# When the weights' high and low planes are made in an encoder block's projections: 20 and 26 products behind the load instead of 24 and 54

## The chip, the cores and the metric

The kernel runs on one core of a Trainium2 chip. Its time is the device time of one execution in microseconds (us). Five engines work side by side, each through its own list of instructions in order, and they wait for each other through semaphores: TensorE (PE in the profile; PEld is its weight load), VectorE (DVE), ScalarE (ACT), GpSimd (POOL) and SyncE (SP), which issues most of the DMAs.

## The reference

One transformer encoder block in float32, for 1024 tokens of width 1024. What matters here is its first half: a layer norm, one wide projection into queries, keys, values and two gates, and two attentions that are computed from it.

```python
h = layer_norm(x, ln0_g, ln0_b)
proj = h @ w_in + b_in                      # 1024 x 1024 times 1024 x 4352
qa, ka, va, qb, kb, vb, ga, gb = split(proj)
y_na = neighbourhood_attention(qa, ka, va, na_rpb) @ w_branch_na     # 8 heads, 16 x 64 grid
y_swa = windowed_gqa_with_sink(rotary(qb), rotary(kb), vb, sink) @ w_branch_swa   # 8 heads, window 128
mixed = sigmoid(ga) * y_na + sigmoid(gb) * y_swa
h = layer_norm(ALPHA * h + mixed @ w_out + b_out, ln1_g, ln1_b)
u = square(relu(h @ w_ff1 + b_ff1))
out = layer_norm(ALPHA * h + u @ w_ff2 + b_ff2, ln2_g, ln2_b)
```

## The kernel before, in words

**Products in two planes.** PE multiplies a rounded type. To keep float32 accuracy, each operand is split into a high plane (the value rounded) and a low plane (value minus high plane), and each product is made as three matmuls: high by high, high by low, low by high. For weights, ScalarE makes the high plane `whi` with a cast (line 550) and VectorE makes the low plane `wlo` with a subtract (line 555).

**Blocks.** The projections are cut into blocks of 128 output columns by all 1024 tokens. A block is 48 products (8 slices of the inner dimension, 3 products each, for two halves of the tokens), issued by `gemm3_steps` (line 282; its matmul is line 288), one for each `next` of a generator. `fills` (line 735) lists the 24 blocks: key, value and first queries of the windowed attention, then its other queries with three gates between, then values, query and key pairs of the neighbourhood heads, and last three more gates. The accumulated 128 x 512 results lie in PSUM under the tag `mm`, two banks, and are evacuated by ScalarE and VectorE.

**Loading a block's weights.** `blocks` (line 539) runs them one behind the other. When a block starts, it forces whatever is not yet made of its own planes, issues the load of the next block's weights (`raw`, 512 KB, two buffers, line 156, on SP's queue) and notes the next block's cast and subtract as deferred steps. `whi` and `wlo` have two buffers each.

```python
            def both():
                split_hi()
                split_lo()
            defer(D_W[0], split_hi, D_W[1], split_lo)
            return both
        force = {0: fetch(0)}
        yield
        for j, (_, run) in enumerate(todo):
            force[j]()
            if j + 1 < len(todo):
                force[j + 1] = fetch(j + 1)
            yield from run(got[j])
```

**Deferred steps.** `defer(n, f, m, g)` (line 295) puts f on a list with a counter of n. `pump` (line 788) issues products and lowers all counters by one for each. `flush` (line 299) runs those whose counter has come to zero, and only then puts g on the list with a counter of m. So m counts from the place where f ran, and a step whose count is up still waits for the next flush. The code is written in the order in which the engines get their instructions; nothing is moved later.

**Where the products run.** The first 188 products (`N_PRE`, line 874) run with a flush after every 4. The others fill the attention's 64 steps and two more: 12 products in a step for the first eight heads (windowed), 18 for the other eight (neighbourhood), 4 steps a head. `steps` (line 849) writes a step s in this order: scores of step s + 2 (`part_a`: four matmuls, lines 606 and 607, into the banks `s` and `t`; VectorE adds the mask and takes the maximum in line 608, then lines 613 or 615), 25% of the products, an early flush for some evacuations, the low half of the probabilities of step s + 1 (`part_l`: VectorE line 643, then a transposing DMA, line 646, into `pt`), exponentials of step s + 2 (`part_e`: ScalarE lines 631 and 634), a flush, 45% of the products, the value matmuls of step s - 1 (`part_c`: line 716 out of `pt`, evacuated by lines 722 and 725), a flush, and the remaining products. With 12 products the parts are 3, 5 and 4, with 18 they are 4, 8 and 6. One rotary operation on GpSimd (lines 458 to 462) is put behind each step's scores while there are any; lines 506 and 511 split its result. Lines 662, 664 and 687 belong to the softmax's normalisation, once for two heads.

After this stage come the rest of the gates, the branch products, the output projection, and the two MLP products (matmuls of lines 1419 and 1852), which the change does not touch.

Of the kernel before, what the change touches and what calls it, by code (L numbers as in the profile page):

```python
# [44 lines left out]

B_V = 8
N_AHEAD = 4
D_W = 24, 30
D_NA = 4
D_ROPE = 4, 22, 8  # L50
D_ROPE2 = 4, 40, 4
# [37 lines left out]
def encoder_block(ctx, tc, x, w_in, w_br, w_out, w_ff1, w_ff2, par, rows, rpbp,  # L89
# [205 lines left out]
    def defer(*fns, pe=False, early=False):  # L295

        later.append([fns[0], fns[1:], pe, early])
# [241 lines left out]
    def blocks(todo):  # L539
# [4 lines left out]
        def fetch(j):  # L544
# [7 lines left out]
            def split_lo():  # L552
                if len(got[j]) == 2:
                    got[j].append(0)
                    W_ENG.tensor_tensor(out=got[j][1], in0=raw, in1=b32(got[j][0]), op=ALU.subtract)  # L555
# [6 lines that stand above are left out]
# [1570 lines left out]
```

## Time and profile before

| | us |
|---|---|
| median of 3 runs (lowest, highest) | 1331.54 (1330.53, 1331.69) |
| the profiled execution, its own time | 1329.35 |
| its span, first to last instruction | 1327.5 |
| PE busy in the span | 1276.8 |
| VectorE, ScalarE, GpSimd busy | 945.8, 708.7, 293.5 |
| stretch from 44 to 450 us: PE busy of 406 | 371.89 |

The mean granted clock of PE over the span was 0.985 of full speed. The stretch from 44 to 450 us holds the projections' blocks and the attention's steps. In the profile's rows, a line number is that of the kernel, `out<-in` names the tiles, `x16` is a count, and what stands behind `<-` in brackets or behind `|` is the idle time just ahead and what ended it. Rows of waits give us in total, times, and the longest. Matmuls overlap: one lasts 0.39 us by the profile and the next starts 0.23 us after it.

### The profile page before, as it was taken

The page shows a single profiled execution, that of the slowest core. Times are in us where ns is not written, and L with a number is a line of the kernel's source. Part 1 is how long each engine was busy: PE and PEld are TensorE (multiplying, and loading weights), DVE is VectorE, ACT ScalarE, POOL GpSimd, SP SyncE. Part 2 cuts the span into 40 slices and gives each one's busy share as a digit, 9 for nine tenths or more (in the row PEclk, how much of TensorE's full clock was granted, in tenths as well). Part 3 has the DMA queues.
Part 4 walks back from the last instruction along what each step waited for, and adds up shares of the span by engine and source line. Part 5 has one row for each costly group of instructions (what it writes and reads, how often), then busy time and mean ns, then how long its engine had stood idle before and what let it go on. Part 6 is the DMA issues. An engine that isn't in the chain of part 4 may idle for free.

```text
span 1327.5 us, 16368 instructions
## 1 busy us (share of the span) xinstructions
PE 1276.8 (96%) x5912; PEld 1042.7 (79%) x5912; DVE 945.8 (71%) x1368; ACT 708.7 (53%) x1148; POOL 293.5 (22%) x279
## 2 busy tenths in 40 slices
PE   8998889899999999999999999999999999999997
PEld 6776767677777878888888888888888888888885
DVE  7766666767776896443688986677655768787778
ACT  6446657666766545541446755555555533333346
POOL 4442220212211000344630012222100001111207
PEclk9999889899999999999999999999999999999998
DMA  6525544555455633655233566565528644544323
GB/s 228 190 95 135 114 122 114 120 120 138 124 111 142 191 131 103 215 194 202 80 143 140 193 222 205 207 207 186 202 96 309 222 191 151 214 151 180 121 104 127
DMA packets 167730, 213.64 MB, mean 161 GB/s; under 512 B 110561, under 2 KB 112353, under 8 KB 161889
## 3 DMA queue, kind: packets, MB, share of 16 engines
q1 hardware_dynamic: 166816, 211.81, 49.2%
q8 instruction: 46, 0.75, 0.2%
q10 hardware_dynamic: 832, 0.79, 0.2%
q14 instruction: 36, 0.29, 0.1%
HBM read 130.69 MB, written 56.18 MB: 141 GB/s over the span
## 4 chain that ended last, share of the span: by engine, by line
PE 84%; DVE 10%; ACT 2%; issue 2%; POOL 1%; DMA 0%; DVEq 0%; POOLq 0%
PE ps_mm L288 17%; PE ps_mm L1419 7%; PE ps_o L1419 6%; PE ps_t L1419 6%; PE ps_mm L1852 6%; PE ps_s L1852 6%; PE ps_o L1852 5%; PE ps_t L1852 5%; PE ps_s L1419 3%; PE ps_o L716 3%; DVE wlo L555 2%; PE ps_mm L949 1%; DVE ss L608 1%; PE ps_s L1310 1%; PE ps_s L1309 1%
## 5 line engine op out<-in xcount | busy, mean ns | idle before, releaser
L288 PE MATMUL ps_mm<-hT,whi 128*128 128x512 f32 x832 | 275.1, 405 | 2.6 <-POOL hT L260 2.1
L288 PE MATMUL ps_mm<-hT,wlo 128*128 128x512 f32 x416 | 170.9, 411 | 35.1 <-DVE wlo L555 34.1
L288 PEld LDWEIGHTS ps_mm<-hT,whi 128*128 128x128 f32 x832 | 159.8, 193 | 35.4 <-POOL hT L260 3.5
L288 PEld LDWEIGHTS ps_mm<-hT,wlo 128*128 128x128 f32 x416 | 80.5, 193 | 54.4 <-DVE wlo L555 41.0
L631 ACT ACTIVATE ss<-ss,sk 128x384 f32<-128x384 f32 (+1 forms) x128 | 74.4, 582 | 80.5 <-DVE sk L613 44.6
L1718 ACT CAST t<-stg 128x2048 fp32r<-128x2048 f32 x28 | 53.5, 1912 | 84.2 <-PE ps_o L1852 46.7
L1871 POOL TENSOR_TENSOR acc<-acc,rst 128x512 f32<-128x512 f32 x16 | 29.5, 1841 | 294.1 <-DMA rst<-xr_d 279.4
L1852 PE MATMUL ps_mm<-t,t 128*128 128x512 f32 x384 | 89.7, 389 | 0.0
L1852 PE MATMUL ps_s<-t,t 128*128 128x512 f32 x384 | 89.6, 389 | 0.0
L1852 PEld LDWEIGHTS ps_s<-t,t 128*128 128x128 f32 x384 | 72.1, 188 | 14.9
L1852 PEld LDWEIGHTS ps_mm<-t,t 128*128 128x128 f32 x384 | 72.1, 188 | 15.0
L1419 PE MATMUL ps_t<-hS,tw 128*128 128x512 f32 x348 | 83.6, 389 | 0.0
L1721 DVE TENSOR_TENSOR t<-stg,t 128x2048 fp32r<-128x2048 f32 x28 | 68.7, 2454 | 13.1 <-ACT t L1718 13.1
L1419 PEld LDWEIGHTS ps_t<-hS,tw 128*128 128x128 f32 x348 | 65.3, 188 | 13.5
L1241 POOL TENSOR_TENSOR mx<-sg 128x512 f32<-128x512 f32 x16 | 33.5, 2091 | 176.3 <-DVE sg L1240 176.3
L1852 PE MATMUL ps_t<-t,t 128*128 128x512 f32 x288 | 67.8, 390 | 0.8 <-DVE t L1721 0.8
L1852 PE MATMUL ps_o<-t,t 128*128 128x512 f32 x288 | 67.2, 389 | 0.0
L1695 POOL TENSOR_TENSOR rst<-rst,rr 128x512 f32<-128x512 f32 x16 | 23.3, 1458 | 188.2 <-DMA rst<-xn_d 118.9
L1852 PEld LDWEIGHTS ps_t<-t,t 128*128 128x128 f32 x288 | 53.9, 188 | 12.7 <-DVE t L1721 1.6
L1852 PEld LDWEIGHTS ps_o<-t,t 128*128 128x128 f32 x288 | 54.1, 188 | 11.2
L643 DVE SCALAR_TENSOR_TENSOR pl<-ss,pl 128x640 f16<-128x640 f32 (+1 forms) x64 | 58.3, 912 | 0.3 <-issue 0.2
L1610 DVE TENSOR_TENSOR usl<-usl 128x512 f32<-128x512 f32 x64 | 50.2, 784 | 11.5 <-ACT usl L1503 10.6
(315 smaller groups left out, 2963.3 us busy)
## 6 DMA issues: line engine op xcount, KB each, us to landing
us_d<-usl SPq DMA_DIRECT2D x112, 256.0 KB, 2.6
stg<-us_d SPq DMA_DIRECT2D x28, 1024.0 KB, 4.9
raw<-in_w_ff SPq DMA_DIRECT2D x36, 512.0 KB, 5.4
raw<-in_w_in SPq DMA_DIRECT2D x28, 512.0 KB, 4.1
sg<-sg_d SPq DMA_DIRECT2D x32, 256.0 KB, 3.3
w2b<-in_w_ff SPq DMA_DIRECT2D x7, 1024.0 KB, 7.0
w2a<-in_w_ff SPq DMA_DIRECT2D x5, 1024.0 KB, 6.9
sg_d<-sa SPq DMA_DIRECT2D x16, 256.0 KB, 2.2
```

The costliest lines, as they stand in the source:

```text
L288: PE.matmul(ps, a[:, k, :], act(b, k), start=(k == 0 and i == 0), stop=(k == NK - 1 and i == 2))
L555: W_ENG.tensor_tensor(out=got[j][1], in0=raw, in1=b32(got[j][0]), op=ALU.subtract)
L631: ACT.activation(p, p, AF.Exp, bias=nm[:, i:i + 1], scale=0.125, accum_out=sums_l[o_chunk][:, hh, 2 * t + i:2 * t + i + 1])
L643: DVE.scalar_tensor_tensor(out=pl[:, n:2 * n], in0=e[:, 0:n], scalar=P_SCALE, in1=pl[:, 0:n], op0=ALU.mult, op1=ALU.subtract)
L716: PE.matmul(o, vs, move(part), start=(m == 0 and part == 0), stop=(m == len(runs) - 1 and part == 1))
L1241: POOL.tensor_tensor(out=mx[:, f, half * 512:(half + 1) * 512], in0=both[0], in1=both[1], op=ALU.add)
L1419: PE.matmul(ps, ww, act[:, part, k, :], start=(first and k == 0 and m == 0), stop=(k == 3 and m == 2), skip_group_check=True)
L1610: DVE.tensor_tensor(out=out, in0=a, in1=b, op=op)
L1718: ACT.copy(slot[:, :, 0, :], src)
L1721: DVE.tensor_tensor(out=slot[:, :, 1, :], in0=src, in1=b32(slot[:, :, 0, :]), op=ALU.subtract)
L1852: PE.matmul(ps, st[:, a, part, j * P:(j + 1) * P], w[:, a, wpart, :], start=(first and a == 0 and m == 0), stop=(a == 3 and m == 2), skip_ ...
L1871: POOL.tensor_tensor(out=z, in0=z, in1=t, op=ALU.add)
```

## The change

One tuple of constants. Its first number counts the products from the issue of a block's load to the cast (high planes), the second those from there to the subtract (low planes).

```diff
-D_W = 24, 30
+D_W = 20, 6
```

The low planes were due 24 + 30 = 54 products behind the load and are now due 20 + 6 = 26 behind it. Everything else is as it was.

## The prediction

> **What bounds the kernel now.** I read the page's totals and chain first, then its groups, then the waits of TensorE, and last the instructions around single waits.
>
> ```profile
> span 1327.5 us, 16368 instructions
> PE 1276.8 (96%) x5912; PEld 1042.7 (79%) x5912; DVE 945.8 (71%) x1368; ACT 708.7 (53%) x1148; POOL 293.5 (22%) x279
> ...
> PE 84%; DVE 10%; ACT 2%; issue 2%; POOL 1%; DMA 0%; DVEq 0%; POOLq 0%
> ...
> L288 PE MATMUL ps_mm<-hT,wlo 128*128 128x512 f32 x416 | 170.9, 411 | 35.1 <-DVE wlo L555 34.1
> ```
>
> PE carries the span: busy 96%, 84% of the chain. 1327.5 - 1276.8 leaves 50.7 us of idle PE, and one group holds 35.1 of it: the products that use a low plane, ended by the subtraction of line 555, which makes that plane. Asked for PE alone, from 44 to 450 us (the stage that D_W governs), the waits give one row only, and the line's own view says how many instructions stand behind it:
>
> ```profile
> PE ps_mm L288 <- DVE wlo L555: 34.1, 16, 3.6
> ...
> L555 DVE TENSOR_TENSOR wlo<-raw,whi x24: 1160/1218/2306, 43.6 to 430.1; 128x1024 fp32r<-128x1024 f32 x24
> ...
> L550 ACT CAST whi<-raw x24: 1031/1037/1056, 42.5 to 425.8; 128x1024 fp32r<-128x1024 f32 x24
> ```
>
> So 16 of 24 blocks of 48 products begin with PE idle, 34.1 us in all. Why does VectorE come late? The subtract is due 24 + 30 = 54 products behind the load, but the next block starts 48 behind it and forces it there, two products before its first use. It then stands in VectorE's order behind everything of that step. Here is VectorE around one such place (start, length, what; in brackets idle before it), then PE:
>
> ```profile
> 166.14 0.95 DVE L643 SCALAR_TENSOR_TENSOR pl<-ss,pl 128x768 f16<-128x768 f32 x1
> 167.02 0.74 DVE L458 STREAM_SHUFFLE qs<-qf 128x512 f32<-128x512 f32 x1
> 168.71 0.42 DVE L608 CUSTOM_DVE_ANT_0 ss<-ps_s,bd 128x256 f32<-128x256 f32 x1 [0.95 <-PE ps_s L607]
> ...
> 169.79 0.82 DVE L643 SCALAR_TENSOR_TENSOR pl<-ss,pl 128x640 f16<-128x640 f32 x1
> 170.53 0.68 DVE L725 TENSOR_TENSOR oT<-ps_o,oT 64x512 f32<-64x512 f32 x1
> 171.13 0.78 DVE L662 TENSOR_TENSOR sl<-sl,sk 128x16 f32<-128x16 f32 x1
> ...
> 172.12 1.16 DVE L555 TENSOR_TENSOR wlo<-raw,whi 128x1024 fp32r<-128x1024 f32 x1
> 177.64 0.56 DVE L608 CUSTOM_DVE_ANT_0 ss<-ps_s,bd 128x384 f32<-128x384 f32 x1 [4.37 <-PE ps_s L607]
> ```
>
> ```profile
> 169.78 0.63 PE L288 MATMUL ps_mm<-hT,whi 128*128 128x512 f32 x2
> 173.33 0.50 PE L288 MATMUL ps_mm<-hT,wlo 128*128 128x512 f32 x1 [2.92 <-DVE wlo L555]
> 176.85 0.52 PE L606 MATMUL ps_s<-kh,q 128*128 128x384 f32 x1
> ```
>
> PE ends its two high-plane products at 170.41 and waits 2.92 us while VectorE works through lines 643, 725 and 662 and then the subtract. Straight after that VectorE itself idles 4.37 us, for PE's next scores: the wait is one of order, not of too much work.
>
> A second cost hangs on these waits. The granted clock, in the windows by stretch (us, busy time of PE, PEld, DVE, ACT, POOL, then PEclk, DMA share, GB/s), and the same few PE instructions after a shorter wait:
>
> ```profile
> 40.00:120.00 80.00, 76.27 (x355) 61.67 (x354) 51.65 (x91) 39.59 (x73) 31.52 (x21) 1.00 0.42 134
> ...
> 120.00:400.00 280.00, 250.33 (x1288) 200.32 (x1286) 196.55 (x435) 183.48 (x376) 58.11 (x80) 0.94 0.51 121
> ```
>
> ```profile
> 110.72 0.50 PE L288 MATMUL ps_mm<-hT,wlo 128*128 128x512 f32 x1 [1.78 <-DVE wlo L555]
> 111.05 0.40 PE L288 MATMUL ps_mm<-hT,whi 128*128 128x512 f32 x1
> ...
> 111.88 0.47 PE L288 MATMUL ps_mm<-hT,whi 128*128 128x512 f32 x1
> ...
> 112.88 0.33 PE L606 MATMUL ps_s<-kh,q 128*128 128x384 f32 x1
> ...
> 215.06 0.80 PE L288 MATMUL ps_mm<-hT,wlo 128*128 128x512 f32 x1 [2.30 <-DVE wlo L555]
> ...
> 236.74 0.80 PE L288 MATMUL ps_mm<-hT,wlo 128*128 128x512 f32 x1 [3.57 <-DVE wlo L555]
> ...
> 257.53 0.50 PE L288 MATMUL ps_mm<-hT,wlo 128*128 128x512 f32 x1 [1.84 <-DVE wlo L555]
> ...
> 338.54 0.50 PE L288 MATMUL ps_mm<-hT,wlo 128*128 128x512 f32 x1 [2.56 <-DVE wlo L555]
> ```
>
> From the released product to the next score matmul PE takes 112.88 - 110.72 = 2.16 us after the 1.78 us wait, and 176.85 - 173.33 = 3.52 us after the 2.92 us one. The released product itself shows 0.80 us instead of 0.50 after waits of 2.30 and 3.57. Waits up to 1.84 us show no slow phase; of those from 2.30 us on, most do (2.56 at 338.54 does not). A clock of 0.94 over 280 us is 0.06 x 280 = 16.8 us lost, if PE was busy throughout the slow phases.
>
> **The change, part by part.** One tuple changes: the cast of a block's weights (line 550, ScalarE) is due 20 products behind the load's issue instead of 24, the subtract (line 555, VectorE) 6 behind the cast instead of 30. No work, wait or buffer is added or removed, and loads are issued where they were.
>
> *Where they land.* Deferred steps run only at flushes. In the attention of the first eight heads a step has 12 products, flushed after 3 and 8. The 188 products ahead of the steps put each block's start at the 4th product of a step, so the flushes lie 4, 11, 16, 23, 28, 35, 40, 47 products behind it. The cast moves from 28 to 23. The subtract moves from the next block's start (48) to 35, behind line 643 of the step before. In the later eight heads (18 products a step, flushed after 4 and 12) block starts rotate over products 4, 16 and 10 of a step: the subtract lands at 36, 32 and 30, the cast at 26, 24 (both as before) and 20 (from 30). In the 188 products ahead the flush comes every 4: cast 20, subtract 28.
>
> *The subtract, on VectorE.* Prices on PE:
>
> ```profile
> 96.12 0.17 PE ps_s L606
> ...
> 96.82 2.76 PE ps_mm L288 x12
> ```
>
> A product costs 2.76 / 12 = 0.230 us, a group of four score matmuls about 4 x 0.17 = 0.7, a group of value matmuls 111.88 - 111.05 - 0.23 = 0.6. The low plane is used two products into the next block, 15 or 16 behind its new place, where it was two behind its old one: it gains at least 13 x 0.230 + 0.7 + 0.6 = 4.3 us. The longest wait is 3.6 us, so VectorE may be as late as it is today and every one of the 16 waits still goes. In the step shown, the subtract would come behind the 166.14 instruction, end near 167.1 + 1.2 = 168.3, and be needed at 170.4. Queued behind it there are the shuffle at 167.02 and then the scores of line 608, which have 0.95 us of idle in front; the rest of the delay ends in the following step, which has lost its subtract.
>
> Does VectorE have the room? The sums over seven blocks of the first eight heads, 109.45 to 256.26 us, over six stretches in them without a PE wait, and the idle ahead of the scores:
>
> ```profile
> sum 146.81, PE 126.27 PEld 99.97 DVE 98.85 ACT 94.31 POOL 30.46; mean PE 18.04 PEld 14.28 DVE 14.12 ACT 13.47 POOL 4.35
> ```
>
> ```profile
> sum 71.95, PE 71.95 PEld 58.26 DVE 52.98 ACT 53.44 POOL 14.56; mean PE 11.99 PEld 9.71 DVE 8.83 ACT 8.91 POOL 2.43
> ```
>
> ```profile
> L608 DVE CUSTOM_DVE_ANT_0 ss<-ps_s,bd 128x384 f32<-128x384 f32 x18 | 10.0, 556 | 33.3 <-PE ps_s L607 33.2
> ```
>
> A block takes 146.81 / 7 = 21.0 us, with (146.81 - 126.27) / 7 = 2.9 of waits and, of the slow clock's loss (15, below), some 12 / 7 = 1.7; without both, 16.4. VectorE has 14.1 us of work in it (86%), ScalarE 13.5 (82%). That is tight, but in the stretches without waits VectorE idles 26% and nearly all its idle time (the 33.2 of the last row) is waiting for PE. So little should come back. Bounds: nothing, or, if VectorE could never be busier than the 52.98 / 71.95 = 74% of those stretches, 14.1 / 0.74 = 19.1 us a block, 2.7 more than 16.4, which over 8 blocks is 21 us. I take 4 us, near the lower end, since its idleness is waiting for PE.
>
> *Contention.* One subtract took 2.31 us beside GpSimd work instead of 1.22:
>
> ```profile
> 56.10 1.74 POOL L461 TENSOR_TENSOR qs<-qs,rt 128x512 f32<-128x512 f32 x1
> ```
>
> ```profile
> 56.62 2.31 DVE L555 TENSOR_TENSOR wlo<-raw,whi 128x1024 fp32r<-128x1024 f32 x1
> ```
>
> The subtract ended 58.93, which is GpSimd's end at 57.84 plus 1.1. At its new place it can meet the rotary operations in the same way; 1.1 us more a block is 15.2 of 16.4 on VectorE, still under, and part of why I do not take nothing.
>
> *The cast, on ScalarE.* It costs 1.04 us wherever it stands and ScalarE has 82% at most, so I cost the move at nothing, if the load has landed:
>
> ```profile
> 172.06 0.57 SPq L156 DMA_DIRECT2D raw<-in_w_in  x1
> ```
>
> ```profile
> raw<-in_w_in SPq DMA_DIRECT2D x24, 512.0 KB, 4.1
> ```
>
> The load is issued some 2 us after PE passed the block's start near 170 (SP's queue stood behind a transpose) and lands 4.1 later, 6.2 us after it; 23 products with two score and two value groups take 5.3 + 1.4 + 1.2 = 7.9. In the 188 products ahead, 20 products are 4.6 us: there the cast may wait a little, with the low plane needed only at product 50 (11.5 us). Behind a waiting cast stand exponentials and evacuations; PE gets them a step later. Bound: 0 to 2 us in all; I take 0.
>
> *The slow clock.* If no wait of 2 us is left, its loss goes too: at least 1.36 us (3.52 - 2.16) for each of some eight phases, 11, and at most 16.8. I take 15, nearer to the clock's own row, as phases go on into the scores that my 1.36 cuts off.
>
> *Sum:* 34.1 + 15 - 4 = 45 us. The profiled execution took 1329.35 us, 1.85 around its span; it would take 1284.3. The median shown, 1331.54, is 2.2 above it: 1286.5.
>
> **Rivals.** *VectorE becomes the bound* of the first eight heads: the 21 us above come back as waits on score banks or again on low planes, and about 28 us are left: 1303. For it: 86% busy, in order, up to 1.1 us of contention a split. Against: VectorE's idle time is PE's lateness.
>
> *The clock does not come back*: gain 34 - 4 = 30, time 1301. The slow phases would then be due to something other than these waits. The Trainium skill, "TensorE: Matmul & The Clock Gate", Part 1, has PE drop to half rate after at least one idle window of about 3.4 us. By that rule only the waits near 3.5 us would have slowed it. The trace differs: the 2.30 and 2.92 us waits were followed by slow products, the waits up to 1.84 were not.
>
> *No change*: the subtract, though issued earlier, is executed as late, because the line 643 in front of it waits for ScalarE: 1331. It would need VectorE over 4.3 us later at the new place than at the old.
>
> *Slower*: the value matmuls become late. Line 643 of a step is followed by a transposing DMA, and its values are used two steps later.
>
> ```profile
> pt<-pl SPq DMA_TRANSPOSE x64, 3.2
> ```
>
> Between are 29 products, two score groups and one value group, 6.7 + 1.4 + 0.6 = 8.7 us; line 643 runs about 2.5 us behind PE, takes 1, the DMA 3.2: 6.7. If the subtract in front of the scores makes VectorE more than 2 us later in every step, and not just in one of four, each us beyond is lost 32 times; from 1.5 us beyond it eats the 45 us, at 2 it adds 64 - 45 = 19: 1350. Against: 14.1 us of work in a 16.4 us block does not pile up.
>
> **How the numbers follow.** Forecast 0.68, VectorE-bound 0.17, clock stays 0.05, no change 0.05, slower 0.05. Time 1286.5. The range: down to all 34.1 + 16.8 = 51 us, 1280; up past the VectorE-bound case's 1303 to 1306, which leaves out the last two cases and some tails. A difference of 0.2% (2.7 us) is about what a measurement here can tell from none. Faster 0.68 + 0.17 + 0.05 = 0.90; same 0.05; slower 0.05.
>
> **What would show it.** Right: no wait of PE on line 555 over 0.3 us; the clock 1.00 in the stretches of the first eight heads; a block of those heads 16 to 17 us; VectorE's share there 83 to 88%; idle ahead of line 608 much shorter. VectorE-bound: PE waiting at lines 606 or 288 on 608 or 555, VectorE above 90%. Clock rival: no waits, clock still below 0.97 there. Wrong altogether: PE waits of 2 us or more on line 555 remaining, or the value matmuls (716) waiting for a DMA.

## The result, and the profile after

| | before | changed |
|---|---|---|
| median (lowest to highest), us | 1331.22 (1330.53 to 1331.69), 4 runs | 1282.34 (1281.79 to 1283.22), 4 runs |
| ratio, 95% interval | | 0.9634 [0.9617, 0.9651] |
| profiled execution, its own time / span, us | 1329.35 / 1327.5 | 1281.79 / 1280.0 |
| PE busy / idle in the span, us | 1276.8 / 50.7 | 1259.9 / 20.1 |

The change saves 48.9 us of the median; 1286.5 was forecast. Measured again later, the changed kernel took 1282.81 us, ratio 0.9639 [0.9626, 0.9652].

The page of the changed kernel: totals, chain, and the two groups of products.

```profile
span 1280.0 us, 16384 instructions
PE 1259.9 (98%) x5912; PEld 1033.1 (81%) x5912; DVE 946.0 (74%) x1368; ACT 707.7 (55%) x1148; POOL 295.2 (23%) x279
...
PE 86%; DVE 7%; ACT 3%; issue 2%; DMA 1%; POOL 1%; SPq 0%; DVEq 0%; POOLq 0%
...
L288 PE MATMUL ps_mm<-hT,whi 128*128 128x512 f32 x832 | 269.8, 399 | 6.3 <-DVE kl L401 3.6
...
L288 PE MATMUL ps_mm<-hT,wlo 128*128 128x512 f32 x416 | 165.6, 398 | 1.0 <-DVE wlo L782 1.0
```

The 35.1 us of idle ahead of the low-plane products are down to 1.0, and that is another line. The products themselves are cheaper on average: 398 ns instead of 411. PE's waits in the stage from 44 to 410 us are again a single row, a new one:

```profile
PE ps_mm L288 <- DVE kl L401: 3.6, 6, 1.0
```

The stage splits at the first scores of the neighbourhood heads. The windows of before (first eight heads, other eight), then of the changed kernel:

```profile
91.10:255.20 164.10, 141.98 (x724) 112.88 (x724) 111.08 (x259) 105.42 (x227) 37.24 (x40) 0.92 0.49 115
255.20:445.50 190.30, 178.62 (x938) 144.16 (x937) 138.94 (x293) 124.63 (x249) 35.26 (x56) 0.98 0.53 129
```

```profile
90.50:220.40 129.90, 128.89 (x723) 105.15 (x722) 109.63 (x259) 104.92 (x227) 39.33 (x40) 1.00 0.64 148
220.40:398.10 177.70, 175.04 (x937) 141.60 (x936) 137.95 (x291) 124.49 (x249) 35.30 (x56) 1.00 0.57 136
```

The first eight heads give 34.2 us, the other eight 12.6, together 46.8 of the span's 47.5. In each half idle PE and busy PE can be told apart: idle fell from 22.1 to 1.0 and from 11.7 to 2.7 us (30.1 in all), busy PE by 13.1 and 3.6 (16.7) with the same products, because the clock rose from 0.92 and 0.98 to 1.00. The other engines did the same work, VectorE 111.08 and then 109.63 us, only in less time.

VectorE and PE at the moved subtract, in the same kind of place as the one shown in the prediction:

```profile
134.07 0.95 DVE L643 SCALAR_TENSOR_TENSOR pl<-ss,pl 128x768 f16<-128x768 f32 x1
134.93 1.22 DVE L555 TENSOR_TENSOR wlo<-raw,whi 128x1024 fp32r<-128x1024 f32 x1
136.18 2.39 DVE L511 TENSOR_TENSOR q<-qf,q 64x512 fp32r<-64x512 f32 x2
138.60 0.42 DVE L608 CUSTOM_DVE_ANT_0 ss<-ps_s,bd 128x256 f32<-128x256 f32 x1
...
139.68 0.82 DVE L643 SCALAR_TENSOR_TENSOR pl<-ss,pl 128x640 f16<-128x640 f32 x1
140.53 0.68 DVE L725 TENSOR_TENSOR oT<-ps_o,oT 64x512 f32<-64x512 f32 x1
```

```profile
138.48 0.40 PE L288 MATMUL ps_mm<-hT,whi 128*128 128x512 f32 x1
138.72 0.83 PE L716 MATMUL ps_o<-pt,vv 128*128 128x256 f16 x8
139.31 0.47 PE L288 MATMUL ps_mm<-hT,whi 128*128 128x512 f32 x1
139.62 0.39 PE L288 MATMUL ps_mm<-hT,wlo 128*128 128x512 f32 x1
```

The subtract now follows line 643 of the step before. VectorE is no earlier against PE than before (line 643 of the next step at 139.68, line 725 at 140.53), but PE goes through its products at 139.31 and 139.62 without a gap.

### The profile page after: what moved, and what is told of

It reads as the page before. It is cut to its first block, busy times and chain, and to the rows that moved or that the text cites. A ratio compares the mean times of both kernels' runs of the same rounds, so it can differ in the third digit from the quotient of the medians.

```text
span 1280.0 us, 16384 instructions
## 1 busy us (share of the span) xinstructions
PE 1259.9 (98%) x5912; PEld 1033.1 (81%) x5912; DVE 946.0 (74%) x1368; ACT 707.7 (55%) x1148; POOL 295.2 (23%) x279
## 4 chain that ended last, share of the span: by engine, by line
PE 86%; DVE 7%; ACT 3%; issue 2%; DMA 1%; POOL 1%; SPq 0%; DVEq 0%; POOLq 0%
PE ps_mm L288 17%; PE ps_mm L1419 7%; PE ps_o L1419 7%; PE ps_t L1419 7%; PE ps_mm L1852 7%; PE ps_s L1852 6%; PE ps_o L1852 5%; PE ps_t L1852 5%; PE ps_s L1419 3%; PE ps_o L716 2%; PE ps_mm L949 2%; PE ps_s L1309 1%; PE ps_s L1310 1%; PE ps_s L1308 1%; PE ps_o L279 1%
## 5 line engine op out<-in xcount | busy, mean ns | idle before, releaser
L288 PE MATMUL ps_mm<-hT,whi 128*128 128x512 f32 x832 | 269.8, 399 | 6.3 <-DVE kl L401 3.6
L288 PEld LDWEIGHTS ps_mm<-hT,whi 128*128 128x128 f32 x832 | 155.3, 188 | 40.7 <-ACT ss L631 3.8
L288 PE MATMUL ps_mm<-hT,wlo 128*128 128x512 f32 x416 | 165.6, 398 | 1.0 <-DVE wlo L782 1.0
L631 ACT ACTIVATE ss<-ss,sk 128x384 f32<-128x384 f32 (+1 forms) x128 | 74.3, 582 | 58.3 <-DVE sk L613 34.1
L288 PEld LDWEIGHTS ps_mm<-hT,wlo 128*128 128x128 f32 x416 | 78.4, 188 | 14.1 <-DVE wlo L782 1.5
L1721 DVE TENSOR_TENSOR t<-stg,t 128x2048 fp32r<-128x2048 f32 x28 | 67.6, 2415 | 13.1 <-ACT t L1718 13.1
```

What stands on the lines that cost most here:

```text
L288: PE.matmul(ps, a[:, k, :], act(b, k), start=(k == 0 and i == 0), stop=(k == NK - 1 and i == 2))
L631: ACT.activation(p, p, AF.Exp, bias=nm[:, i:i + 1], scale=0.125, accum_out=sums_l[o_chunk][:, hh, 2 * t + i:2 * t + i + 1])
L1721: DVE.tensor_tensor(out=slot[:, :, 1, :], in0=src, in1=b32(slot[:, :, 0, :]), op=ALU.subtract)
```

## The experiments

My theory was that the whole gain comes from the subtract's place in VectorE's order, directly as waits and through the clock that the waits pull down. The rivals: the earlier cast takes part in it; VectorE's load, not its order, sets the time; the slow clock has another cause. Every edit is shown against the kernel before, unless it says otherwise.

**The cast alone.**

```diff
-D_W = 24, 30
+D_W = 20, 34
```

> The cast alone at 20, the subtract still due 54 behind the load, so still forced at the next block's start. Theory (the whole gain is the subtract's place in VectorE's order): no change, 1331 us within 1.5, PE's waits on line 555 still about 34 us in 16 places, the slow clock still there. Rival (the earlier high planes carry part of the gain, as VectorE's subtract can only start behind the cast): 1320 to 1328 us, shorter waits on line 555.

Measured: 1331.39 us, ratio 1.0006 [0.9996, 1.0015]. PE's waits:

```profile
PE ps_mm L288 <- DVE wlo L555: 34.5, 16, 3.6
```

Same waits, same time: the cast's number has no part in the gain.

**The subtract alone.**

```diff
-D_W = 24, 30
+D_W = 24, 6
```

> The cast as before at 24, the subtract 6 behind it. Theory: the whole gain, 1281 to 1283 us; no wait of PE on line 555. In the later heads the cast of one block in three goes back from 20 to 30 products, so ScalarE no longer waits for the load (6.5 us in the changed kernel), and PE's waits on line 401 (3.6 us there) fall to 2 us or less: perhaps 1 us faster than the changed kernel. Rival (both parts are needed): 1285 to 1300 us.

Measured: 1283.54 us, ratio 0.9652 [0.9637, 0.9666], not to be told from the changed kernel's 0.9634. The whole gain, then, but not the 1 us more that I expected; the time lies just above the theory's 1281 to 1283. ScalarE's 6.5 us of waits for loads are gone, but PE's waits on line 401 fell only from 3.6 to 2.8 us, and two small ones on line 555, where I expected none, remain:

```profile
PE ps_mm L288 <- DVE kl L401: 2.8, 4, 1.1
...
PE ps_mm L288 <- DVE wlo L555: 0.8, 2, 0.5
```

**One flush later.**

```diff
-D_W = 24, 30
+D_W = 20, 13
```

> The subtract 13 instead of 6 behind the cast: in the first eight heads it runs 40 products into the block instead of 35, still ahead of the scores of the step in which the next block starts; in the later heads at 44, 42 and 38. Theory (what counts is that it stands ahead of that step's work in VectorE's order): as the changed kernel, 1282 us within 2, no wait on line 555 over 0.5 us. Rival (only the time by which it is moved ahead comes off each wait, here 8 products and a score group, 2.5 us): 1286 us or more, with waits of 0.3 to 1 us left in six blocks of the first eight heads.

Measured: 1297.16 us, ratio 0.9752 [0.9735, 0.9768]: 15 us slower than the changed kernel and above the theory's 1282 within 2. The rival's "1286 us or more" covers it, but most of the loss is not where the rival had it. The waits on line 555, one of them on PE, and VectorE around it:

```profile
PE ps_mm L288 <- DVE wlo L555: 10.8, 8, 2.6
```

```profile
259.84 0.51 PE L288 MATMUL ps_mm<-hT,wlo 128*128 128x512 f32 x1 [2.56 <-DVE wlo L555]
```

```profile
257.83 0.82 DVE L643 SCALAR_TENSOR_TENSOR pl<-ss,pl 128x640 f16<-128x640 f32 x1
258.57 1.22 DVE L555 TENSOR_TENSOR wlo<-raw,whi 128x1024 fp32r<-128x1024 f32 x1
```

Three waits of 2.56 us stand in the later heads, where I expected none. I had overlooked that for one block in three the flush at 42 lies in the step in which the next block starts, behind that step's line 643. There the wait is 2.56 us, exactly as in the kernel before, although the subtract is issued 6 products earlier. That is the strongest evidence for order: six products buy nothing as long as the same instruction stands in front. In the first eight heads and at their end four small waits are left (0.47 to 0.92 us), fewer than the rival's six, more than the theory's none; there this run does not decide between the two.

**Two flushes later.**

```diff
-D_W = 24, 30
+D_W = 20, 18
```

> The subtract 18 behind the cast: in the first eight heads it runs 47 products into the block, one product ahead of the forced place, behind line 643 of the step in which the next block starts; in the later heads still early, at 44, 42 and 38. Theory: in the first eight heads all waits come back (the nine from 94 to 258 us sum to 24.0 us) with six of the eight slow phases (about 13 us), in the later heads none: 1282.3 + 24 + 13 = 1319 us within 4. Rival (the slow clock and the waits in one part of the stage come from elsewhere, or VectorE's load and not the order makes them): a time near 1282 or near 1331, or waits in both parts.

Measured: 1313.75 us, ratio 0.9877 [0.9862, 0.9892], a little under the 1315 to 1323 of the theory. That it came so near is luck: the theory had 24 us of waits in the first eight heads and none in the later ones, and of the 23.4 us measured, 7.7 are three waits of 2.56 us in the later heads. There the subtract lands at 42 again in one block in three, the place that I overlooked in the run before; waits in both parts were what the rival named. The waits in all, one of them, and VectorE in front of it:

```profile
PE ps_mm L288 <- DVE wlo L555: 23.4, 13, 2.7
```

```profile
167.03 0.51 PE L288 MATMUL ps_mm<-hT,wlo 128*128 128x512 f32 x1 [1.40 <-DVE wlo L555]
```

```profile
165.02 0.82 DVE L643 SCALAR_TENSOR_TENSOR pl<-ss,pl 128x640 f16<-128x640 f32 x1
165.75 1.22 DVE L555 TENSOR_TENSOR wlo<-raw,whi 128x1024 fp32r<-128x1024 f32 x1
166.89 0.68 DVE L725 TENSOR_TENSOR oT<-ps_o,oT 64x512 f32<-64x512 f32 x1
167.49 0.65 DVE L662 TENSOR_TENSOR sl<-sl,sk 128x16 f32<-128x16 f32 x1
```

The subtract comes one product before its forced place, but in the flush it goes ahead of lines 725 and 662, which stood in front of it before. The wait here is 1.40 us where it was 2.92 at the same kind of block start. The difference, 1.5, is about what the two instructions that changed sides took, 0.68 + 0.78. So at this place the wait is, piece by piece, what stands in front of the subtract from line 643 on.

**Filler on PE, no subtract moved.** The kernel before, with eight matmuls in front of nine blocks' first product; they write the bank that this product then starts anew.

```diff
+        filler = 8 if n_half[0] in range(13, 13 + 18, 2) else 0
...
+                for _ in range(filler if k == 0 and i == 0 else 0):
+                    PE.matmul(ps, hi[:, 0, :], act(0, 0), start=True, stop=True)
```

> The kernel before, with 8 filler matmuls (1.84 us) on PE ahead of the first product of the nine blocks that start from 93 to 258 us; they write the bank that the block's first product then overwrites. The low planes are as late as before, so PE is held up to the same moment, only busy instead of idle. Theory (idle PE makes the slow clock): waits left of at most 1.8 us, no slow phase in these blocks, and the 12 to 14 us of slow clock of the first eight heads come back without any subtract being moved: 1318 us within 3. Rival (the slow phases have another cause): 1331 us, or up to 1348 if the fillers do not fit into the waits (9 x 1.84 = 16.6 us more).

Measured: 1319.65 us, ratio 0.9913 [0.9898, 0.9927]: 11.9 us faster, with 72 matmuls more and no operand earlier. The windows of the two halves (the low planes' line is 561 here):

```profile
91.00:244.40 153.40, 145.58 (x788) 117.05 (x788) 111.10 (x259) 105.31 (x227) 37.95 (x40) 1.00 0.55 124
244.40:435.00 190.60, 180.39 (x944) 145.58 (x944) 138.39 (x292) 124.51 (x249) 34.94 (x56) 0.98 0.53 129
```

With the gaps filled, the first half runs at clock 1.00 (0.92 before) and takes 153.4 us instead of 164.1; the second half, with fillers only at its very start (the last of the nine blocks), keeps its 0.98 and its 190 us. That idle PE pulls the clock down is shown for the first eight heads.

**Each subtract twice.** The changed kernel, with the moved subtract written two times.

```diff
                     W_ENG.tensor_tensor(out=got[j][1], in0=raw, in1=b32(got[j][0]), op=ALU.subtract)
+                    W_ENG.tensor_tensor(out=got[j][1], in0=raw, in1=b32(got[j][0]), op=ALU.subtract)
```

> The changed kernel with each of the moved subtracts made twice: 1.22 us more work on VectorE in each of 24 blocks, 29 us in all, and nothing else. Theory (VectorE has room: 14.1 + 1.2 = 15.3 us of 16.4 in a block of the first eight heads): at most 5 us more, 1282 to 1287. Rival (VectorE is now the bound there): most of the 8 to 10 us of the first eight heads and some of the rest comes through, 1292 to 1311 us, with waits of PE on VectorE's lines.

Measured: 1297.5 us, ratio 0.9747 [0.9731, 0.9763]. Of the 29 us added to VectorE 15 come through; my theory allowed 5, and the rival has the time right. The waits and the two halves:

```profile
PE ps_mm L288 <- DVE kl L401: 11.7, 8, 2.0
PE ps_mm L288 <- DVE wlo L556: 3.0, 4, 1.9
```

```profile
92.40:228.00 135.60, 130.30 (x720) 104.18 (x719) 120.36 (x269) 104.97 (x228) 38.62 (x40) 1.00 0.62 142
228.00:412.60 184.60, 175.08 (x938) 141.56 (x936) 151.15 (x302) 124.37 (x249) 36.09 (x56) 1.00 0.53 131
```

The first half is 5.7 us longer and the second 6.9, though VectorE is busy only 89% and 82% of them, so it is not simply full. In the later heads it is again a matter of what stands in front. VectorE and then PE at one place, where PE waited 0.30 us in the changed kernel:

```profile
271.40 1.22 DVE L556 TENSOR_TENSOR wlo<-raw,whi 128x1024 fp32r<-128x1024 f32 x1
...
273.99 0.76 DVE L401 SCALAR_TENSOR_TENSOR kl<-ps_mm,prm,kh 64x512 fp32r<-64x512 f32 x1
```

```profile
274.89 0.70 PE L288 MATMUL ps_mm<-hT,whi 128*128 128x512 f32 x2 [1.34 <-DVE kl L401]
```

The second subtract delays line 401, and PE waits there.

**Evacuations earlier.** The changed kernel, with one more flush of the early evacuations at the end of a step.

```diff
             flush()
-            pump(part[2])
+            pump(part[2]); flush(False, True)
```

> The changed kernel, with one more flush of the early evacuations at the end of a step: in two of three blocks of the later heads, lines 399 and 401, which free a projection's bank, then stand ahead of the next step's scores on VectorE and, in one of them, ahead of the moved subtract. Theory (the 3.6 us of waits on line 401 that the change left behind come from the place of line 401 behind the subtract and the scores): those waits go, 1279 us, 2 to 4 us faster than the changed kernel. Rival (line 401 is late because ScalarE's evacuation is late, so the new order only makes VectorE idle in front of the scores): no gain, or up to 10 us slower.

Measured: 1298.55 us, ratio 0.9754 [0.9741, 0.9767]; 16 us slower than the changed kernel. VectorE, and then PE, at one of the places:

```profile
264.53 0.74 DVE L399 SCALAR_TENSOR_TENSOR q<-ps_mm,prm,q 64x512 fp32r<-64x512 f32 x1 [3.66 <-ACT kh L396]
265.29 0.76 DVE L401 SCALAR_TENSOR_TENSOR kl<-ps_mm,prm,kh 64x512 fp32r<-64x512 f32 x1
...
266.54 0.96 DVE L643 SCALAR_TENSOR_TENSOR pl<-ss,pl 128x768 f16<-128x768 f32 x1
267.42 1.22 DVE L555 TENSOR_TENSOR wlo<-raw,whi 128x1024 fp32r<-128x1024 f32 x1
```

```profile
266.20 0.70 PE L288 MATMUL ps_mm<-hT,whi 128*128 128x512 f32 x2 [1.51 <-DVE kl L401]
268.69 0.50 PE L288 MATMUL ps_mm<-hT,wlo 128*128 128x512 f32 x1 [1.79 <-DVE wlo L555]
```

VectorE stands 3.66 us before line 399, waiting for ScalarE's evacuation of line 396, and line 643 and the subtract stand behind it. Here lines 399 and 401 are late because ScalarE is, not because of their place: the rival, at more than the price that I gave it. In the changed kernel too, line 399 stands waiting for ScalarE; from the view of that line there:

```profile
  ACT kh L396: 7.7, 7
```

**Still earlier.** The changed kernel with

```diff
-D_W = 20, 6
+D_W = 20, 1
```

> The subtract due 1 instead of 6 products behind the cast: in the first eight heads it runs 28 products into the block instead of 35, in the later heads where the changed kernel has it. Theory (once it stands ahead of the next block's first step nothing more is to be had): as the changed kernel within 1.5 us, 1281 to 1284. Rival (VectorE's order matters at every place, also in the step before): a difference of 3 us or more either way, with new waits of PE on other lines of VectorE.

Measured: 1287.14 us, ratio 0.9669 [0.9656, 0.9682], 4.3 us slower than the changed kernel beside it. The rival again:

```profile
PE ps_mm L288 <- DVE kl L401: 6.4, 7, 1.9
```

```profile
217.99 1.23 DVE L555 TENSOR_TENSOR wlo<-raw,whi 128x1024 fp32r<-128x1024 f32 x1 [1.73 <-ACT whi L550]
219.13 0.55 DVE L608 CUSTOM_DVE_ANT_0 ss<-ps_s,bd 128x384 f32<-128x384 f32 x1
...
221.19 0.74 DVE L399 SCALAR_TENSOR_TENSOR q<-ps_mm,prm,q 64x512 fp32r<-64x512 f32 x1
221.95 0.76 DVE L401 SCALAR_TENSOR_TENSOR kl<-ps_mm,prm,kh 64x512 fp32r<-64x512 f32 x1
```

Too close behind the cast, the subtract waits for ScalarE (1.73 us) at the head of VectorE's queue, with the scores and then line 401 behind it.

**The changed kernel again**, beside the two runs just told.

> The changed kernel itself, on the chip of the two runs beside it, as their measure: 1282 us within 1.5.

Measured: 1282.81 us. The runs with one and two flushes later also move the subtract in the later heads, so their medians mix two places. The starts of line 608 part them: from the first scores to the first of the neighbourhood heads, and from there to the last scores.

| subtract in the first eight heads at | median, us | first eight heads, us | other eight, us |
|---|---|---|---|
| 28 products (still earlier) | 1287.14 | 132.8 | 173.7 |
| 35 (changed kernel) | 1282.34 | 130.0 | 171.8 |
| 40 (one flush later) | 1297.16 | 133.4 | 182.4 |
| 47 (two flushes later) | 1313.75 | 147.7 | 184.6 |
| 48 (before) | 1331.22 | 164.1 | 184.4 |

At 28, 35 and 40 products the first eight heads differ by 3.4 us at most. In the other eight, one flush later loses 10.6 of the 12.6 us gained there, and two flushes later all of them. No version tried beats the changed kernel.

## Why the prediction was right, point by point

- *The waits on line 555 go* (34.1 us): right, none is left on PE.
- *What comes back* (4 us, on VectorE in the first eight heads): the size was right, the place wrong, so the agreement is luck. It is 3.6 us at line 401, the evacuation that frees a projection's bank, five of the six waits in the stretch of the later heads. The first eight heads keep 1.0 us of idle PE.
- *The slow clock* (15 us): 16.9 us by PE's busy time. The row of the clock, 16.8, was the better price than the 11 that I pulled the estimate towards. The filler run shows the cause for the first eight heads: with the clock at 1.00 they take 10.7 us less, the fillers' own time included. The rival that the clock would stay low falls.
- *A block of the first eight heads at 16 to 17 us, VectorE at 83 to 88%*: 129.9 / 8 = 16.2 us, and 109.63 / 129.90 = 84%.
- *Where the steps land*: right for the subtract. Wrong for the cast: I had it move from 28 to 23 in the first eight heads. The product that starts a block lowers the new counter at once, so a count of 24 is up at product 23, and the cast ran there before too. It moves from 30 to 20 in three blocks of the later heads, and from 24 to 20 in the four blocks loaded during the first 188 products. No term hung on it.
- *The cast costs nothing*: right on PE. ScalarE does now wait for the load, far longer than the 2 us that I allowed, but the run with the subtract alone, without these waits, is no faster. Of 6.5 us, 6.3 are in the three blocks whose cast moved from 30 to 20; I had timed the load against the first eight heads and the 188 products ahead, not against these blocks.

```profile
ACT whi L550 <- DMA raw<-in_w_in: 6.5, 4, 2.5
```

- *VectorE has the room* (14.1 of 16.4 us, 26% idle and waiting for PE): the argument was too generous. It held for the moved work, but the doubled subtract shows half of its added work coming through. The idle time ahead of line 608 did become much shorter, 13.6 us after 45.7 in the first eight heads. Idle time that waits for PE in one place is no reserve in another, since VectorE takes its list in order. My bound of 21 us given back, which made the VectorE-bound rival, was the right kind of caution.
- *No change*, if VectorE were over 4.3 us late at the new place: it did not happen, and the two later flushes show where it would have, in the step that starts the next block.
- *Contention*, a part of why I did not take nothing: it did not come there. At the new place each subtract of the first eight heads took 1.22 us.
- *Slower*: PE's waits in this stage hold no row for the value matmuls of line 716.

With the forecast of 45 us against 48.9, the difference is 1.9 us of clock, 0.4 of waits, and the rest outside this reckoning: the profiled pair differs by 47.6 us, the medians by 48.9.

## What to carry to other kernels

Where one engine waits for another that is far from busy, look at what stands ahead of the awaited instruction in that engine's own list: here the wait was made of those instructions, and moving the subtract past them took it away, while issuing it six products earlier behind the same instruction did not. Such a step has two bad ends: too late it stands behind the next step's work, too early it blocks the queue while it waits for its own input. Count the slow clock after PE's gaps as part of their price, half as much again here.

## What the runs showed of the hardware

Gaps of PE pulled its clock down without a sharp limit. In the run with the subtract still earlier, PE's clock over six us around two waits of similar length:

```profile
204.57 0.70 PE L288 MATMUL ps_mm<-hT,whi 128*128 128x512 f32 x2 [1.76 <-DVE kl L401]
...
222.85 0.70 PE L288 MATMUL ps_mm<-hT,whi 128*128 128x512 f32 x2 [1.89 <-DVE kl L401]
```

```profile
204.00:210.00 6.00, 5.43 (x31) 4.34 (x32) 5.80 (x16) 4.17 (x10) 0.00 (x0) 1.00 0.85 201
222.00:228.00 6.00, 5.14 (x21) 3.88 (x22) 5.80 (x14) 5.49 (x12) 1.27 (x2) 0.72 0.95 229
```

After 1.76 us the clock stayed at 1.00, after 1.89 it fell to 0.72. It is not the length alone. In the run with two flushes later, 1.77 us before 109.34 were followed by 7 us at a mean clock of 0.76; in the run with each subtract twice, 1.99 us before 266.03 left the clock at 1.00, and so did 2.56 us before 338.54 in the kernel before. The Trainium skill, "TensorE: Matmul & The Clock Gate", Part 1, has PE drop to half rate after at least one idle window of about 3.4 us, and calls the window free-running. The rows here show slow phases after gaps of about half of that. A free-running window would fit that the length of a gap does not decide alone; no run here tested it.
